# Forward attention of a gated recurrence sent through DRAM and added to the backward one, so that one product with the values serves both directions

## The chip, the core and the metric

The kernel runs on one core of a Trainium2 chip. The engines are named as in the profile: PE (TensorE, matrix products), PEld (its weight loads), DVE (VectorE), ACT (ScalarE), POOL (GpSimd) and SP (SyncE, which here issues nearly all DMA transfers). The metric is the device time of one execution in microseconds (us); lower is better.

## What is computed

One layer of a block with two recurrent branches over 2048 latent tokens and 256 context tokens, model width 1024. The change lies in the second branch (HGRN2, branch B), which has 4 heads of width 128 and runs over the sequence in both directions; the outputs of the two directions are added:

```python
def step(S, inp):                       # one chunk of one direction
    qg_c, attn_c, v_c, kd_c, gl_c = inp
    o_c = einsum('bhcd,bhdv->bhcv', qg_c, S) + einsum('bhcs,bhsv->bhcv', attn_c, v_c)
    S = S * gl_c[..., :, None] + einsum('bhcd,bhcv->bhdv', kd_c, v_c)
    return S, o_c
...
for d in range(2):                      # forward, then backward
    o_c, o_l = prefix_scan(gla_chunk_scan, ctx_args, lat_args, s0_b, reverse=(d == 1))
    ob_lat_cm = ob_lat_cm + o_l
```

Within a chunk the output is a part from the state S that came in, and a part `attn . v` from the chunk's own tokens. `attn` is lower triangular in the forward direction and upper triangular in the backward one; v is the same in both. So attn_forward . v + attn_backward . v = (attn_forward + attn_backward) . v.

## The kernel before

The program has these stages in order of time: the modulated input (0 to 170 us of the span), the projections with convolution of branch A (to about 500 us), the whole of branch B (about 500 to 1046 us), the preparation of branch A's chunks (to about 1450 us), branch A's recurrence (to about 1700 us), and the output with its projections and normalisation (to the end). Gate projections, which depend on nothing in the recurrences, are spread among the last three. All projections are products of 128 x 512 tiles in float32r, each done as three products of high and low halves (lines L216 to L218, tile `ps`).

Branch B is the function `scan_group(h, d, g, ps, S)`, called per head h (4), direction d (0 forward, 1 backward) and group g of 512 tokens: four latent groups and one context group of 256 tokens (g = 4), which comes first in both directions and has no output. The chunk is 128 tokens, so a latent group has k_ = 4 of them, index i. One latent group does, in short: gates on ACT and DVE (tiles `s`, `sn`, `X`; the running sum is L546, with the mask `m32` as one operand), scaled queries and keys `ag`, `bg`, `a64`, `b64`, `b32` (L601 and L619 on DVE, L604, L620, L621 on POOL), the transposed keys `pk` and `kd`, the state updates' products `pS` (L614), the chunk's attention in 32 x 32 and 32 x 64 pieces into the PSUM tile `pat` (L625, L627), and then

- L647, DVE: the allowed triangle of `pat` is copied into `atB[d]`, an SBUF tile per direction whose other triangle is zero;
- L655, PE: `pw` = queries times state S (queries `ag` forward, `bg` backward);
- L656, PE: `pw` += `atB[d]` times v, four products of 128 x 128 in float32;
- L661, DVE: the next state, in a ring of four tiles of tag "S";
- forward: ACT copies `pw` to `o` (L664), and SP stores it to the DRAM tensor `oP` (L665); backward: SP loads `oP` into `o` (L650), DVE adds `pw` (L667), and SP stores the sum (L668).

A group's values v are loaded from DRAM into the single tile `v` (L588), the queries into the single tile `q` (L591). Between groups, `head_units` (values and queries of the next head) and `gate_units` are called as filling; their projections are what PE does while a group's chain runs on the other engines.

The order of the instructions on each engine isn't the order of the code: a scheduler (`schedule_with_timeline_sim=True`) simulates the program while it is built and lays down each engine's list. Each engine then executes its list strictly in order, and so does SP with its DMA issues: an instruction that waits holds up all that stand behind it on its engine. Tiles come from pools; a tile that is used again waits for the last reader of its earlier use.

Of the kernel before, what the change touches and what calls it, by code (L numbers as in the profile page):

```python
# [8 lines left out]
F32 = mybir.dt.float32  # L9
F32R = mybir.dt.float32r  # L10
U8 = mybir.dt.uint8
AF = mybir.ActivationFunctionType
ALU = mybir.AluOpType
# [3 lines left out]
P = 128  # L17
# [7 lines left out]
H = 4  # L25
# [3 lines left out]
NG = SEQ // GT  # L29
# [10 lines left out]
def block_kernel(ctx, tc, x, c, ctx_in, c_ctx, w_mod, b_mod, w_in, conv_w, a_log, dt_bias,  # L40
                 lb_param, a_norm_g, b_norm_g, w_a_out, w_b_out, w_out, ln_g, ln_b, out, dbg=None):
    nc = tc.nc
    sy, te, ve, ac, po = nc.sync, nc.tensor, nc.vector, nc.scalar, nc.gpsimd
# [43 lines left out]
    dr = ctx.enter_context(tc.tile_pool(name="dr", reuse_waits="tile", bufs=1, space=DRAM))  # L87
# [62 lines left out]
    qB = dr.tile([H, NG, P, GT], F32, name="qB")  # L150
    vB = dr.tile([H, NG + 1, P, 4, P], F32, name="vB")
    oP = dr.tile([H, NG, P, 4, P], F32, name="oP")
    oBD = dr.tile([SEQ // P, P, H, P], F32, name="oBD")
    gateD = dr.tile([1, D], F32, name="gateD")
    gT = dr.tile([24, P, SEQ], F32, name="gT")
# [55 lines left out]
    def proj(w, gi, pool=None, tag="pj"):  # L211
        wh, wl = w
        n = GT if gi < NG else CTX
        ps = (pool or pj[0]).tile([P, n], F32, tag=tag, name="ps")
        for k in range(KB):
            te.matmul(out=ps, lhsT=wh[:, k, :], rhs=uhi[gi][:, k, :], start=(k == 0), stop=False)  # L216
            te.matmul(out=ps, lhsT=wh[:, k, :], rhs=ulo[gi][:, k, :], start=False, stop=False)  # L217
            te.matmul(out=ps, lhsT=wl[:, k, :], rhs=uhi[gi][:, k, :], start=False, stop=(k == KB - 1))  # L218
        return ps
# [15 lines left out]
    with tc.tile_pool(name="w0", reuse_waits="tile", bufs=1, side="right") as w0, \  # L235
# [85 lines left out]
        for k in range(KB):  # L321
            if k in (0, 2):
                w_part(w0_, gcol[0], 2 * k)
            for j in range(2):
# [4 lines left out]
                for i in range(2):  # L329
                    te.matmul(out=pm[2 * j + i], lhsT=sc[:, k, :], rhs=wm[:, i * 512:i * 512 + 512],  # L330
                              start=(k == 0), stop=(k == KB - 1))
# [176 lines left out]

    with tc.tile_pool(name="rb", reuse_waits="tile", bufs=1, side="right") as rb, \
            tc.tile_pool(name="pb", reuse_waits="tile", bufs=1, space=PSUM) as pb:  # L510
        m32 = rb.tile([P, 256], F32, name="m32")
        po.memset(m32, 1.0)
        po.memset(m32.rearrange("p (b t) -> p b t", t=32)[:, :, 0:1], 0.0)
        mk = [rb.tile([P, P], U8, name=f"mk{d}") for d in range(2)]
        atB = [rb.tile([P, 4, P], F32, name=f"atB{d}") for d in range(2)]
# [6 lines left out]
        def bl(a):  # L522
            return slice(32 * a, 32 * a + 32)

        def b4(t):
            return t.rearrange("p c (b t) -> p c b t", t=32)

        def scan_group(h, d, g, ps, S):
# [25 lines left out]
            else:  # L554
                ve.tensor_tensor(out=X3[:, :, 1:32], in0=s3[:, :, 0:31],
                                 in1=s3[:, :, 15:16].to_broadcast([P, nb, 31]), op=ALU.subtract)
# [30 lines left out]
            v = rb.tile([P, 4, P], F32, tag="v", name="v")  # L587
# [7 lines left out]
            def fb(f, m):  # L595
                return f.unsqueeze(3).to_broadcast([P, k_, m, 32])
# [18 lines left out]
            if lat:  # L615
                a64 = rb.tile([P, 4, 64], F32, tag="a64", name="a64")
                b64 = rb.tile([P, 4, 64], F32, tag="b64", name="b64")
                b32 = rb.tile([P, 4, 64], F32, tag="b32", name="b32")
                ve.tensor_tensor(out=b4(a64), in0=b4(a)[:, :, 2:4], in1=fb(f2, 2), op=ALU.mult)  # L619
                po.tensor_tensor(out=b4(b64), in0=b4(b)[:, :, 0:2], in1=fb(f3, 2), op=ALU.mult)  # L620
                po.tensor_tensor(out=b4(b32), in0=b4(b)[:, :, 0:4:2], in1=fb(f4, 2), op=ALU.mult)  # L621

                def mm(i, am, bm, asl, bsl):
                    if d == 0:
                        te.matmul(out=pat[bsl, i, asl], lhsT=bm, rhs=am, start=True, stop=True)  # L625
                    else:
                        te.matmul(out=pat[asl, i, bsl], lhsT=am, rhs=bm, start=True, stop=True)  # L627


                def across32(i, k):  # L630
                    mm(i, a[:, i, bl(2 * k + 1)], b32[:, i, bl(k)], bl(2 * k + 1), bl(2 * k))

                def across64(i, k):
                    if d == 0:
                        mm(i, a64[:, i, :], b64[:, i, bl(k)], slice(64, 128), bl(k))
                    else:
                        mm(i, a64[:, i, bl(k)], b64[:, i, :], bl(2 + k), slice(0, 64))

                for i in range(4):
                    for k in range(4):  # L640
                        mm(i, a[:, i, bl(k)], b[:, i, bl(k)], bl(k), bl(k))
                for i in range(4):
                    across32(i, d)
                    across32(i, 1 - d)
                    across64(i, d)
                    across64(i, 1 - d)
                ve.copy_predicated(out=atB[d], mask=mk[d].unsqueeze(1).to_broadcast([P, 4, P]), data=pat)  # L647
                o = rb.tile([P, 4, P], F32, tag="o", name="o")
                if d == 1:
                    sy.dma_start(out=o, in_=oP[h, g])  # L650
                pw = pb.tile([P, 4, P], F32, tag="o", name="pw")
                qg = ag if d == 0 else bg
            for i in (range(k_) if d == 0 else range(k_ - 1, -1, -1)):
                if lat:
                    te.matmul(out=pw[:, i, :], lhsT=qg[:, i, :], rhs=S, start=True, stop=False)  # L655
                    te.matmul(out=pw[:, i, :], lhsT=atB[d][:, i, :], rhs=v[:, i, :], start=False, stop=True)  # L656
                S2 = rb.tile([P, P], F32, tag="S", name="S2", bufs=4)
                if S is None:
                    ve.tensor_copy(out=S2, in_=pS[:, i, :])
                else:  # L660
                    ve.scalar_tensor_tensor(out=S2, in0=S, scalar=fz[:, i, 14:15], in1=pS[:, i, :], op0=ALU.mult, op1=ALU.add)  # L661
                S = S2
            if lat and d == 0:
# [43 lines left out]
        for h in range(H):  # L707
            fill = head_units(h + 1) if h + 1 < H else gate_units(NEARLY + GA)
            for d in range(2):
                w = load_w((C_FF, C_FB)[d] + h * P)  # L710
                S = None
                for j, g in enumerate(((4, 0, 1, 2, 3), (4, 3, 2, 1, 0))[d]):
                    S = scan_group(h, d, g, proj(w, g), S)
                    for _ in range(FBI[d][j] if h + 1 < H else FB[j] * d):
                        next(fill, None)
            for _ in fill:
                pass
# [18 lines left out]
    with tc.tile_pool(name="rc", reuse_waits="tile", bufs=2, side="right") as rc, \  # L736
# [8 lines left out]
        for d in range(2):  # L745
            po.tensor_copy(out=after[d].rearrange("p (h t) -> p h t", h=H),
                           in_=(m_lt, m_gt)[d].bitcast(F32).unsqueeze(1).to_broadcast([P, H, P]))
# [192 lines left out]
    if True:  # L940
# [9 lines left out]
        def stepA(d, ch, lat, second, last):  # L950
# [14 lines left out]
            def mm4(lhs, rhs):  # L965
                cnt[0] += 1
                two = cnt[1] >= SW and cnt[0] % 3
                ps = (pd2 if two else pd).tile([P, H, P], F32, tag="A", name="psA")
                for h in range(H):
                    te.matmul(out=ps[:, h, :], lhsT=lhs[:, h, :], rhs=rhs[:, h, :], start=True, stop=True)  # L970
                return ps

            def tok_scale(tag, ps, sc_):
                t = rd.tile([P, H, P], F32, tag=tag, name=tag)
                for h in range(H):
                    ac.activation(out=t[:, h, :], in_=ps[:, h, :], func=AF.Copy, scale=sc_[:, d, ch, h:h + 1])
                return t
# [7 lines left out]
            if not last:  # L985
                pS = mm4(kn, tok_scale("vx", pv, nbze))
                S2 = rd.tile([P, H, P], F32, tag=f"S{d}", name="S2")
                for h in range(H):
                    ve.scalar_tensor_tensor(out=S2[:, h, :], in0=S[:, h, :], scalar=gl[:, d, ch, h:h + 1], in1=pS[:, h, :],  # L989
                                            op0=ALU.mult, op1=ALU.add)  # L990
                SA[d] = S2
            if lat:
# [242 lines left out]
```

## Time and profile before

| what | us |
|---|---|
| median of 3 runs | 2251.22 (2248.89 to 2253.9) |
| the profiled execution | 2248.18 |
| its span, first to last instruction | 2246.4 |
| PE busy in it | 2134.7 (95%) |
| DVE, ACT, POOL busy | 1395.4 (62%), 927.1 (41%), 655.3 (29%) |
| DMA engines, hardware queue | 48.0% of 16 engines' span |

The profile is one execution. "Busy" is the time in which an engine has an instruction of the program in execution. Records of matrix products overlap one another (each is in flight for longer than the distance to the next one), so the distance between two starts is what one costs PE; a product in float32 shows as two records. Names stand as out<-in without buffer numbers. The lines of the profile are shown in the prediction, at the place where each is used.

### The profile page before, as it was taken

The numbers are of one execution on the slowest core, as the hardware profiler recorded it, in microseconds if no ns is written. First come the engines' busy times: TensorE is split into PE (matmuls) and PEld (weight loads), VectorE is DVE, ScalarE is ACT, GpSimd is POOL, SyncE is SP. The second block draws the span as 40 slices with busy tenths as digits, with TensorE's granted clock in tenths as the row PEclk, the third lists the DMA queues.
The fourth block names the chain that finished last, engine by engine and source line by source line (L and its number), as shares of the span: only waits on it lengthen the run. The fifth ranks groups of instructions, "written<-read, shape, count | busy, mean of one in ns | idle before, by whom it ended". The sixth has DMA issues, their size and how long they took to land. (4 is left out here: it accounts for less than half of the span.)

```text
span 2246.4 us, 40304 instructions
## 1 busy us (share of the span) xinstructions
PE 2134.7 (95%) x15184; PEld 1786.2 (80%) x15184; DVE 1395.4 (62%) x3225; ACT 927.1 (41%) x2334; POOL 655.3 (29%) x656
## 2 busy tenths in 40 slices
PE   8999999999999999999998898999989888999998
PEld 3778888888888888888777677788778877888887
DVE  5836666627776777784698887733332338666664
ACT  4623222224443443443455554344444445444441
POOL 3413343312221222223333332211133224423331
PEclk9999999999999999999999999999999999999999
DMA  8312222322322323225778887777878864444432
GB/s 338 109 39 71 68 73 69 92 71 69 97 83 76 106 69 97 83 86 160 237 221 234 246 242 203 241 208 223 236 260 288 267 210 154 141 137 127 140 95 80
DMA packets 303670, 339.77 MB, mean 151 GB/s; under 512 B 78124, under 2 KB 217650, under 8 KB 303476
## 3 DMA queue, kind: packets, MB, share of 16 engines
q1 hardware_dynamic: 301459, 329.87, 48.0%
q0 software_dynamic: 2016, 7.34, 0.9%
q8 instruction: 119, 1.95, 0.4%
q14 instruction: 76, 0.61, 0.1%
HBM read 226.27 MB, written 110.87 MB: 150 GB/s over the span
## 5 line engine op out<-in xcount | busy, mean ns | idle before, releaser
L216 PE MATMUL ps<-uhi,wh 128*128 128x512 f32 (+1 forms) x1824 | 708.4, 388 | 4.2 <-DVE uhi L305 2.0
L217 PE MATMUL ps<-ulo,wh 128*128 128x512 f32 (+1 forms) x1824 | 708.0, 388 | 2.9 <-DVE ulo L310 1.7
L218 PE MATMUL ps<-uhi,wl 128*128 128x512 f32 (+1 forms) x1824 | 707.3, 388 | 0.7 <-POOL wl L203 0.7
L216 PEld LDWEIGHTS ps<-uhi,wh 128*128 128x128 f32 x1824 | 346.3, 190 | 68.5 <-DVE uhi L305 3.0
L217 PEld LDWEIGHTS ps<-ulo,wh 128*128 128x128 f32 x1824 | 346.1, 190 | 66.2 <-DVE ulo L310 2.5
L218 PEld LDWEIGHTS ps<-uhi,wl 128*128 128x128 f32 x1824 | 346.2, 190 | 63.3 <-POOL wl L203 1.1
L203 POOL TENSOR_TENSOR wl<-ws,wh 128x512 fp32r<-128x512 f32 x144 | 192.8, 1339 | 590.5 <-ACT wh L202 575.1
L202 ACT CAST wh<-ws 128x512 fp32r<-128x512 f32 x144 | 89.3, 620 | 292.8 <-DMA ws<-in_w_in_dram 214.3
L418 DVE SCALAR_TENSOR_TENSOR acc<-raw,cols,acc 128x512 f32<-128x512 f32 x192 | 153.9, 854 | 0.9
L1134 PE MATMUL py<-yh,wab 128*128 128x256 f32 x512 | 145.0, 284 | 7.5 <-DVE mg L1137 6.0
L1135 PE MATMUL py<-yl,wab 128*128 128x256 f32 x512 | 144.4, 282 | 1.4 <-POOL yl L1117 1.4
L1136 PE MATMUL py<-yh,wab 128*128 128x256 f32 x512 | 143.7, 281 | 0.0
L604 POOL TENSOR_TENSOR bg<-s,fz 128x512 f32<-128x512 f32 (+1 forms) x36 | 37.5, 1041 | 260.9 <-ACT X L584 106.7
L1153 PE MATMUL pso<-uhi,mh 128*128 128x512 f32 x256 | 102.9, 403 | 8.0 <-ACT mh L1139 4.1
L1134 PEld LDWEIGHTS py<-yh,wab 128*128 128x128 f32 x512 | 96.8, 190 | 10.0 <-DVE mg L1137 7.4
L1155 PE MATMUL pso<-uhi,ml 128*128 128x512 f32 x256 | 101.8, 398 | 0.6 <-DVE ml L1140 0.6
L1154 PE MATMUL pso<-ulo,mh 128*128 128x512 f32 x256 | 101.4, 397 | 0.0
L1135 PEld LDWEIGHTS py<-yl,wab 128*128 128x128 f32 x512 | 97.0, 189 | 2.3 <-POOL yl L1117 1.8
L1136 PEld LDWEIGHTS py<-yh,wab 128*128 128x128 f32 x512 | 97.5, 190 | 0.1
L989 DVE SCALAR_TENSOR_TENSOR S<-S,gl,psA 128x128 f32<-128x128 f32 x136 | 38.2, 341 | 87.0 <-PE psA L970 87.0
L1117 POOL TENSOR_TENSOR yl<-gt,yh 128x512 fp32r<-128x512 f32 x32 | 44.9, 1405 | 147.4 <-ACT yh L1116 147.4
L1127 ACT ACTIVATE mg<-mg 128x512 f32<-128x512 f32 x64 | 40.4, 632 | 112.2 <-DMA mg<-gT 106.5
(373 smaller groups left out, 3963.1 us busy)
## 6 DMA issues: line engine op xcount, KB each, us to landing
ws<-in_w_in_dram SPq DMA_DIRECT2D x144, 256.0 KB, 3.0
gT<-gt SPq DMA_DIRECT2D x96, 256.0 KB, 4.4
kv<-knvD SPq DMA_DIRECT2D x36, 512.0 KB, 5.9
kq<-qkvD SPq DMA_DIRECT2D x32, 512.0 KB, 5.5
an<-atN SPq DMA_DIRECT2D x32, 512.0 KB, 6.2
mg<-gT SPq DMA_DIRECT2D x64, 256.0 KB, 3.4
qkvD<-acc SPq DMA_DIRECT2D x48, 256.0 KB, 2.3
l<-qkvD SPq DMA_DIRECT2D x16, 768.0 KB, 6.1
```

The lines of the kernel that those rows point to most:

```text
L202: ac.copy(out=wh[:, j:j + 4, :], in_=ws)
L203: po.tensor_tensor(out=wl[:, j:j + 4, :], in0=ws, in1=wh[:, j:j + 4, :].bitcast(F32), op=ALU.subtract)
L216: te.matmul(out=ps, lhsT=wh[:, k, :], rhs=uhi[gi][:, k, :], start=(k == 0), stop=False)
L217: te.matmul(out=ps, lhsT=wh[:, k, :], rhs=ulo[gi][:, k, :], start=False, stop=False)
L218: te.matmul(out=ps, lhsT=wl[:, k, :], rhs=uhi[gi][:, k, :], start=False, stop=(k == KB - 1))
L418: ve.scalar_tensor_tensor(out=a_, in0=raw[:, o + k:o + k + n], scalar=wk, in1=a_, op0=ALU.mult, op1=ALU.add)
L1134: te.matmul(out=py[:, i, :], lhsT=wh[:, k, ms_], rhs=yh[i][:, k, :], start=(k == 0), stop=False)
L1135: te.matmul(out=py[:, i, :], lhsT=wh[:, k, ms_], rhs=yl[i][:, k, :], start=False, stop=False)
L1136: te.matmul(out=py[:, i, :], lhsT=wl[:, k, ms_], rhs=yh[i][:, k, :], start=False, stop=(k == H - 1))
L1153: te.matmul(out=ps, lhsT=mh[:, k, ts_], rhs=wout[0][k][:, ns], start=(k == 0), stop=False)
L1154: te.matmul(out=ps, lhsT=mh[:, k, ts_], rhs=wout[1][k][:, ns], start=False, stop=False)
L1155: te.matmul(out=ps, lhsT=ml[:, k, ts_], rhs=wout[0][k][:, ns], start=False, stop=(k == KB - 1))
```

## The change

In the forward direction the product `atB[0]` . v is left out: `pw` holds the state's part alone. Instead SP stores `atB[0]` to a new DRAM tensor `atF` (256 KB for each of 16 head and group pairs). In the backward direction SP loads it into a new tile `at`, POOL adds `atB[1]` to it in place, and PE multiplies the sum with v. To make room for `at`, the mask `m32` becomes uint8 and the ring of states has three tiles in place of four.

```diff
+    atF = dr.tile([H, NG, P, 4, P], F32, name="atF")
...
-        m32 = rb.tile([P, 256], F32, name="m32")
+        m32 = rb.tile([P, 256], U8, name="m32")
...
                 ve.copy_predicated(out=atB[d], mask=mk[d].unsqueeze(1).to_broadcast([P, 4, P]), data=pat)
+
+                if d == 0:
+                    sy.dma_start(out=atF[h, g], in_=atB[0])
+                else:
+                    at = rb.tile([P, 4, P], F32, tag="at", name="at")
+                    sy.dma_start(out=at, in_=atF[h, g])
+                    po.tensor_tensor(out=at, in0=at, in1=atB[1], op=ALU.add)
                 o = rb.tile([P, 4, P], F32, tag="o", name="o")
...
             for i in (range(k_) if d == 0 else range(k_ - 1, -1, -1)):
                 if lat:
-                    te.matmul(out=pw[:, i, :], lhsT=qg[:, i, :], rhs=S, start=True, stop=False)
-                    te.matmul(out=pw[:, i, :], lhsT=atB[d][:, i, :], rhs=v[:, i, :], start=False, stop=True)
-                S2 = rb.tile([P, P], F32, tag="S", name="S2", bufs=4)
+                    te.matmul(out=pw[:, i, :], lhsT=qg[:, i, :], rhs=S, start=True, stop=d == 0)
+                    if d == 1:
+                        te.matmul(out=pw[:, i, :], lhsT=at[:, i, :], rhs=v[:, i, :], start=False, stop=True)
+                S2 = rb.tile([P, P], F32, tag="S", name="S2", bufs=3)
```

The new lines make all later line numbers larger: up to L645 by one, then more. The product with v is L665 in the changed kernel (L656 before), the product with the state L663 (L655), the state update L670 (L661), the addition on POOL L655, the store and the load of `atF` L651 and L654.

The scheduler lays the lists down anew. Only the stage of branch B and the stages of branch A's preparation and the first half of its recurrence come out in another order; what is ahead of branch B, and the rest of the recurrence and the output, stand as before. Three places are shown.

PE, a forward group of the first head, around the products with the state. `ps` is projection work of another unit, `S2` the states. Before:

```order
L218 MATMUL ps_4414<-uhi3_634,wl_3892 128x512
L655 MATMUL pw_4084<-S2_4087,ag_4028 128x128
L656 MATMUL pw_4084<-v_4023,atB0_3558 128x128
L655 MATMUL pw_4084<-S2_4091,ag_4028 128x128
L656 MATMUL pw_4084<-v_4023,atB0_3558 128x128
L655 MATMUL pw_4084<-S2_4095,ag_4028 128x128
L656 MATMUL pw_4084<-v_4023,atB0_3558 128x128
L625 MATMUL pat_3560<-X_4130,s_4128 32x32
L609 MATMUL pk_4166<-ident_60,bg_4164 128x128 x4
```

PE at the same place, now:

```order
L218 MATMUL ps_4406<-ulo3_636,wh_3892 128x512
L663 MATMUL pw_4086<-S2_4088,ag_4029 128x128
L219 MATMUL ps_4406<-uhi3_635,wl_3893 128x512
L217 MATMUL ps_4406<-uhi3_635,wh_3892 128x512
L663 MATMUL pw_4086<-S2_4091,ag_4029 128x128
L626 MATMUL pat_3561<-X_4128,s_4126 32x32
L663 MATMUL pw_4086<-S2_4094,ag_4029 128x128
L626 MATMUL pat_3561<-X_4128,s_4126 32x32 x2
L610 MATMUL pk_4164<-ident_60,bg_4162 128x128 x4
```

The products with v are gone from between the products with the states, and pieces of projection and attention stand there in their place.

POOL, the second and third backward group of the first head. `wl` is the low half of projection weights, which needs ACT's high half and that in turn a weight load; `b64`, `b32` and `bg` are scaled operands of the group. Before:

```order
L604 TENSOR_TENSOR bg_4930<-s_4893,fz_4896 128x512
L620 TENSOR_TENSOR b64_4945<-s_4893,fz_4896 128x256
L621 TENSOR_TENSOR b32_4946<-s_4893,fz_4896 128x256
L203 TENSOR_TENSOR wl_5176<-ws_5181,wh_5175 128x512
L604 TENSOR_TENSOR bg_5101<-s_5064,fz_5067 128x512
L620 TENSOR_TENSOR b64_5116<-s_5064,fz_5067 128x256
L621 TENSOR_TENSOR b32_5117<-s_5064,fz_5067 128x256
```

POOL at the same place, now:

```order
L655 TENSOR_TENSOR at_4975<-at_4975,atB1_3560 128x512
L204 TENSOR_TENSOR wl_5455<-ws_5456,wh_5454 128x512
L605 TENSOR_TENSOR bg_5096<-s_5059,fz_5062 128x512
L621 TENSOR_TENSOR b64_5111<-s_5059,fz_5062 128x256
L622 TENSOR_TENSOR b32_5112<-s_5059,fz_5062 128x256
L204 TENSOR_TENSOR wl_5455<-ws_5460,wh_5454 128x512
L655 TENSOR_TENSOR at_5149<-at_5149,atB1_3560 128x512
```

The addition of the second group follows straight on that group's operands; that of the third stands behind a `wl`. Of the 16 additions 5 stand straight behind a `wl`.

DVE, the end of a backward group of the second head, with its four state updates. Before:

```order
L661 SCALAR_TENSOR_TENSOR S2_6379<-S2_6222,fz_6287,pS_6330 128x128
L661 SCALAR_TENSOR_TENSOR S2_6383<-S2_6379,fz_6287,pS_6330 128x128
L661 SCALAR_TENSOR_TENSOR S2_6387<-S2_6383,fz_6287,pS_6330 128x128
L661 SCALAR_TENSOR_TENSOR S2_6391<-S2_6387,fz_6287,pS_6330 128x128
L562 MEMSET fz_6629 128x4
L546 SCALAR_TENSOR_TENSOR s_6455<-m32_3553,s_6455 128x256 x2
```

The end of that list now, from the next group's last preparing step on (the first three updates stand 15 to 18 rows ahead of it):

```order
L584 TENSOR_TENSOR X_6449<-X_6449,sn_6448 128x512
L594 TENSOR_TENSOR s_6447<-q_6479,s_6447 128x512
L670 SCALAR_TENSOR_TENSOR S2_6383<-S2_6379,fz_6276,pS_6319 128x128
L676 TENSOR_TENSOR o_6366<-o_6366,pw_6368 128x512
L602 TENSOR_TENSOR ag_6482<-X_6449,fz_6450 128x512
```

The fourth update has moved behind nearly all of the next group's gate work: with three tiles its tile is free only after PE's second product with a state of that group.

## The prediction

> **What bounds the kernel now.** I began with the busy time by stage, since the change lies in one of them. In a row of this view stand the stretch in us, its length, then for each engine its busy time and, in brackets, its instructions; at the end TensorE's granted clock, the DMA engines' busy share and GB/s. The first row is branch B, the second branch A's preparation, the third the recurrence.
>
> ```profile
> 514.00:1046.00 532.00, 526.84 (x4714) 446.17 (x4713) 381.51 (x1039) 217.60 (x396) 131.47 (x136) 1.00 0.30 89
> 1046.00:1450.00 404.00, 365.23 (x2686) 298.27 (x2685) 316.31 (x842) 198.94 (x659) 124.76 (x148) 0.96 0.78 232
> 1450.00:1700.00 250.00, 233.02 (x2251) 197.56 (x2249) 85.41 (x263) 110.26 (x350) 53.32 (x70) 0.97 0.77 235
> ```
>
> In branch B PE is without work for 5 us of 532, at the full clock. DVE is busy for 72% of it, POOL for 25%, the DMA engines for 30%. So a product that PE is spared there should be time gained, as long as PE goes on finding work. Busy records of PE overlap, though, so I looked next at what a product costs from start to start, in the timeline (start, duration, line):
>
> ```profile
> 521.39 0.40 PE L217 MATMUL ps<-ulo,wh 128*128 128x512 f32 x1
> 521.63 0.38 PE L656 MATMUL pw<-v,atB 128*128 128x128 f32 x2
> 521.77 0.48 PE L218 MATMUL ps<-uhi,wl 128*128 128x512 f32 x1
> 522.08 0.40 PE L216 MATMUL ps<-uhi,wh 128*128 128x512 f32 x1
> 522.32 0.40 PE L217 MATMUL ps<-ulo,wh 128*128 128x512 f32 x1
> ...
> 523.47 0.38 PE L655 MATMUL pw<-S,ag 128*128 128x128 f32 x2
> 523.69 0.39 PE L656 MATMUL pw<-v,atB 128*128 128x128 f32 x2
> 523.92 0.39 PE L655 MATMUL pw<-S,ag 128*128 128x128 f32 x2
> 524.14 0.39 PE L656 MATMUL pw<-v,atB 128*128 128x128 f32 x2
> ```
>
> In a row of float32 products each starts 0.22 to 0.23 us after the one before. Between projections it costs the same: from 521.39 to 522.08 are 0.69 us, of which two projection products at 0.23 are 0.46, which leaves 0.23 for the one of L656. PE is issuing without a gap, and this is the price.
>
> Then the stage by halves of a head, forward (first and third row and so on) and backward in turn, in stretches of 70 us:
>
> ```profile
> 500.00:570.00 70.00, 70.00 (x623) 60.04 (x622) 51.26 (x160) 31.65 (x59) 13.18 (x15) 1.00 0.24 73
> 570.00:640.00 70.00, 70.00 (x611) 59.29 (x610) 50.62 (x121) 27.65 (x49) 19.51 (x18) 1.00 0.36 104
> 640.00:710.00 70.00, 68.85 (x615) 58.61 (x615) 49.31 (x152) 31.26 (x58) 13.70 (x15) 1.00 0.22 69
> 710.00:780.00 70.00, 70.00 (x611) 59.27 (x610) 49.07 (x114) 27.69 (x50) 19.50 (x18) 1.00 0.34 100
> 780.00:850.00 70.00, 68.18 (x607) 58.14 (x606) 50.34 (x150) 30.20 (x57) 13.65 (x15) 0.98 0.24 73
> 850.00:920.00 70.00, 70.00 (x611) 59.28 (x610) 50.37 (x126) 28.48 (x51) 19.51 (x18) 1.00 0.34 99
> 920.00:990.00 70.00, 67.81 (x649) 56.30 (x648) 59.29 (x170) 32.16 (x60) 16.39 (x18) 1.00 0.24 72
> ```
>
> All that PE misses, it misses in the forward stretches, 1.15, 1.82 and 2.19 us of the third, fifth and seventh row. That is where the products go away. The backward stretches are full, and there the new addition comes in. Last, who waits for whom in the stage (total us, times, longest):
>
> ```profile
> PE pw L655 <- DVE S L661: 2.7, 3, 1.3
> PEld pw L655 <- DVE S L661: 2.5, 2, 1.4
> POOL wl L203 <- ACT wh L202: 119.0, 22, 12.4
> DVE S L661 <- PE pS L614: 11.7, 15, 2.6
> ```
>
> PE's waits on the states come to 5.2 us, nearly all that it waits for; POOL stands for long before a `wl`.
>
> **The change part by part.** *Forward products left out.* 4 heads x 4 groups x 4 chunks are 64 products, half of those in this row (two records each):
>
> ```profile
> L656 PE MATMUL pw<-v,atB 128*128 128x128 f32 x256 | 49.5, 275 | 0.0
> ```
>
> 64 x 0.223 us = 14.3 us less of PE's time. The mean of 275 ns in the row is flight time, which overlaps; it isn't the price. The page "Perfetto Trace Analysis" of the Trainium skill, section "Identifying the Most-Contended Engine", would have PE judged by its weight loads' busy share and not by the products': here 446.17 of 532 us, 84%, so by this rule PE had room and sparing it would bring less. The timeline disagrees: a 512-wide product takes 0.23 us and its load 0.19, so loads can't fill such a stretch while the products do:
>
> ```profile
> L216 PEld LDWEIGHTS ps<-uhi,wh 128*128 128x128 f32 x1824 | 346.3, 190 | 68.5 <-DVE uhi L305 3.0
> ```
>
> *The store and load of `atF`, the addition, `v`.* The nearest rows:
>
> ```profile
> L997 POOL TENSOR_TENSOR o<-o,part 128x512 f32<-128x512 f32 x16 | 20.4, 1276 | 53.3 <-ACT o L976 22.3 <-DMA part<-oAD 12.7 <-DVE r L982 4.7
> L647 DVE COPY_PREDICATED atB<-mk,pat x32: 718/735/747, 518.0 to 1026.9; 128x512 f32<-128x512 uint8 x32
> v<-vB SPq DMA_DIRECT2D x32, 256.0 KB, 2.7
> oP<-o SPq DMA_DIRECT2D x16, 256.0 KB, 3.2
> L650 SPq DMA_DIRECT2D o<-oP x16: 319/320/332, 564.1 to 1030.0; - x16
> ```
>
> L997 is the same operation, in place, on the same shape: 1.28 us. Sixteen are 20.4 us on POOL, in backward stretches where POOL is busy 19.5 of 70. What they stand before is PE's first product with v. In the new order some 17 projection products, four transposes and four products for the state lie between the group's last piece of attention and it: 17 x 0.23 + 8 x 0.2 = 5.5 us. The chain takes 0.74 (L647) + 1.28, with a few tenths for semaphores 2.4 us. Cover is left, 3 us: 0. Without cover it would be 16 x 2.4 = 38 us at most, 0 at least. The load waits, like that of `v` ahead of it on SP, for the last product of the group before; 0.64 us of two issues and 2.7 to land are 3.4 us, and PE comes back to that place after about 12 us: 0. The store makes the next group's L647 wait until it has landed, 0.32 + 3.2 us of a group period of over 10: 0. SP issues 32 transfers more, 32 x 0.32 = 10 us in 532, and 8.4 MB more move at 30% DMA load: 0. The first backward group reads what the last forward one wrote; the context group lies between: 0.
>
> POOL's additions can also stretch DVE. Of these two products, each with two operands in SBUF, the second is always the same, while the first, which runs beside POOL's scaling, goes up to 1.58 us (its minimum is the half size):
>
> ```profile
> L601 DVE TENSOR_TENSOR ag<-X,fz x36: 425/831/1581, 512.5 to 1020.0; 128x512 f32<-128x512 f32 x32, 128x256 f32<-128x256 f32 x4
> L593 DVE TENSOR_TENSOR X<-q,X x16: 676/684/695, 510.3 to 961.1; 128x512 f32<-128x512 f32 x16
> ```
>
> 16 additions x (1.58 - 0.68) = 14 us of DVE at most, 3.6 us in each backward stretch, where DVE has 20 us to spare: 0 on the path. The page "SBUF — State Buffer", section "Who interferes with whom", says that such a DVE instruction and a GpSimd one that reads SBUF lock each other out for a whole instruction; the trace agrees, 1.58 against 0.68 us.
>
> *The mask as uint8.* L546 with a float32 mask, and the scan of branch A, which has a uint8 operand and twice the length:
>
> ```profile
> L546 DVE TENSOR_TENSOR_SCAN s<-m,s x72: 658/682/950, 500.0 to 1013.3; 128x256 f32<-128x256 f32 x72
> L797 DVE TENSOR_TENSOR_SCAN dec<-gb,after x36: 1198/1225/1868, 1048.3 to 1365.6; 128x512 f32<-128x512 f32 x36
> ```
>
> 1225 ns for twice 682 less one fixed part: no dearer. 0, bounds 0 to 72 x 0.05 = 4 us of DVE.
>
> *Three states in place of four.* The fourth update of a group must wait for PE's second product with a state, and stands later on DVE; PE's first product of the next group waits for it. Backward some 7 us of other PE work lie between, forward only the attention pieces and four transposes, about 2 us, for one update of 0.34 us and what DVE has in hand. Lower bound 0, upper bound that the present 5.2 us of waits double, +5.2. I take +2.6: the forward cover is thin and DVE's work in a stretch stays while PE's shrinks by 3.6 us.
>
> *Order in the preparation and recurrence.* PE does the same work there, in another order, and waits 38.8 us of 404, in waits such as these:
>
> ```profile
> PE pkk L805 <- ACT kv L769: 9.6, 8, 1.8
> PE pk L766 <- DMA l<-qkvD: 5.1, 4, 1.6
> ```
>
> That is some 40 waits of 1 us. If each falls anew the sum moves by about the root of 40, 6 us, either way. I take 0, bounds -6 and +6.
>
> *Sum.* -14.3 + 0 + 2.6 + 0 = -11.7 us. The profiled execution took 2248.18 us (span 2246.4 and 1.8 around it), 3.0 less than the median of the runs, so it goes to 2236.5 and the median to 2239.5.
>
> **The rivals.** *A, the spared time becomes waiting.* In the forward stretches the chain over DVE and ACT is close behind: PE already misses 1 to 2 us in three of four there, and the seventh row has DVE busy for 59 of 70. If the chain sets the pace of a forward half, PE's 14.3 us are idle in place of busy: 0 to -4, time about 2249. For it: all waits lie there. Against: DVE has 19 to 21 us to spare in the other rows, and filling work exists. The rule on weight loads above would lead here as well.
>
> *B, the addition is late (slower).* POOL's list puts 5 of 16 additions straight behind a `wl`, and such an instruction has waited up to 12.4 us, 5.4 in the mean, with all behind it. If those five came late by 5.4 us more than the 3 us of cover, and all others by 1, then 27 + 11 - 14.3 = +24 us, 2275. It decides from 0.9 us of wait a backward group (14.3 / 16). For it: the long row. Against: most of those waits are POOL with nothing else to do, and the `wl` ahead of an addition is the second half of a load, whose weights tile is free already.
>
> *C, the new order behind branch B.* It costs 12 us or more in the two later stages, twice what I allow: 2251 or above; or it brings as much, 2227 or less. The trace of before can't say.
>
> **How the numbers follow.** The forecast, -5 to -19 us, has 0.62. A has 0.14 (within 0.2%, 4.5 us, which is about what a measurement of this kernel can tell from no change, as its three runs lie within 5.0 us). B 0.07. C with a cost 0.09, of which 0.04 still comes out slower and 0.05 the same; C with a gain 0.08. So faster 0.62 + 0.08 + 0.01 of the edges = 0.71, same 0.14 + 0.05 - 0.01 = 0.18, slower 0.07 + 0.04 = 0.11. The range: 2227 is 2251.2 - 14.3 - 6 and a run's spread of 4; 2253 takes in A and the mild side of C, and leaves out B. The likeliest case alone: 2232 to 2246.
>
> **What would show it.** Right: branch B's stage some 10 to 14 us shorter, PE's products of L665 half as many as L656's, PE still without work for under 2% of the stage; POOL's additions at 1.28 us with no PE wait on them; the stretch behind branch B as long as now within 6 us. Wrong: PE waiting on `S` of L670 or on ACT's and DVE's gate steps for over 8 us (A), PE waiting on `at` (B), or the preparation longer by more than was gained (C).

## The result, and the profile after

| what | us |
|---|---|
| changed kernel, median of 6 runs | 2232.98 (2229.54 to 2237.38) |
| kernel before beside it, median of 6 runs | 2250.05 (2245.27 to 2253.9) |
| ratio after / before | 0.9932 [0.9916, 0.9948] |
| profiled executions, before and after | 2248.18 and 2233.26 (spans 2246.4 and 2231.6) |

The change makes the kernel 15.3 us faster (11.7 to 18.9 by the interval; the two medians lie 17.1 us apart, within it); forecast were 11.7. The sum came out near. Two of its terms did not, and they partly cancel, which is luck.

The busy time by stage, in the same columns as in the prediction, cut at the same events in both kernels: branch B from its first attention piece to its last `pw`, then the middle (branch A's preparation and the start of its recurrence, up to its last product of `lvt`), the rest of the recurrence, and the output. Before:

```profile
514.50:1039.40 524.90, 519.74 (x4680) 440.31 (x4680) 380.17 (x1036) 216.40 (x393) 125.89 (x127) 1.00 0.30 88
1039.40:1637.30 597.90, 551.29 (x4630) 453.50 (x4628) 384.55 (x1051) 284.50 (x930) 163.01 (x208) 0.97 0.77 228
1637.30:1812.00 174.70, 156.79 (x1016) 141.50 (x1013) 54.14 (x164) 75.38 (x245) 54.33 (x43) 0.96 0.81 267
1812.00:2246.40 434.40, 405.45 (x2530) 358.93 (x2529) 274.08 (x452) 175.07 (x476) 142.47 (x97) 0.99 0.42 134
```

and after:

```profile
515.50:1028.70 513.20, 503.22 (x4533) 424.23 (x4533) 389.86 (x1036) 215.16 (x393) 152.46 (x148) 0.99 0.34 106
1028.70:1626.70 598.00, 549.59 (x4648) 452.49 (x4648) 384.85 (x1051) 283.77 (x930) 162.76 (x204) 0.98 0.76 229
1626.70:1797.90 171.20, 153.77 (x1016) 139.29 (x1013) 54.47 (x165) 75.04 (x245) 54.34 (x43) 0.98 0.83 271
1797.90:2231.60 433.70, 406.90 (x2530) 360.52 (x2529) 274.36 (x452) 175.59 (x476) 143.44 (x97) 0.98 0.42 134
```

Branch B is 11.7 us shorter, just the forecast, what comes behind it 4.1 us shorter, what is ahead 1.0 longer. But the stage doesn't hold the same work: some projections have moved behind it. The same stretches for the first of the three projection lines alone (L216 before, L217 after) show how many:

```profile
514.50:1039.40 524.90, 209.03 (x547) 102.92 (x546) 1.00 0.30 88
```

```profile
515.50:1028.70 513.20, 207.38 (x541) 102.13 (x540) 0.99 0.34 106
```

Six or seven fewer of that line, so about 20 fewer of the three lines, at the 0.23 us from start to start that the prediction read: 4.6 us. At equal work branch B gained 11.7 - 4.6 = 7.1 us, about half of what the spared products are worth, and the middle gained 4.5.

What took the other half? PE is busy for 503.22 of 513.20 us, so it is without work for 10.0 us against 5.2 before, and the granted clock is 0.99 against 1.00. PE's waits on others, after (total us, times, longest; a wait shows only where a releaser is seen):

```profile
PE pat L626 <- POOL b L622: 1.9, 3, 0.8
PE pw L663 <- DVE S L670: 1.7, 2, 1.0
PE pk L610 <- POOL bg L605: 1.7, 3, 1.0
PE pS L615 <- DMA v<-vB: 1.6, 1, 1.6
```

and before:

```profile
PE pw L655 <- DVE S L661: 2.7, 3, 1.3
PE pk L609 <- POOL bg L604: 0.9, 1, 0.9
PE pat L625 <- ACT s L577: 0.9, 1, 0.9
```

The wait on the states went down, with three tiles. What came are waits on POOL's operands, 3.6 us against 0.9, and, in rows not shown, 3.7 us on DVE's `ag` and on the load of `v`, against 0.6. And the clock drops near some of the pauses. PE at the start of the second head, after, in slices of 5 us (length, busy, granted clock, DMA share, GB/s):

```profile
645.00:650.00 5.00, 5.00 (x29) 1.00 0.01 3
650.00:655.00 5.00, 2.87 (x47) 0.88 0.34 107
655.00:660.00 5.00, 5.00 (x47) 0.50 0.01 4
660.00:665.00 5.00, 5.00 (x25) 0.94 0.45 157
```

PE misses 2.1 us, and in this slice and the next two it gets less than its clock: 0.12 + 0.50 + 0.06 of 5 us, 3.4 us more. So the clock that is lost around a pause can be more than the pause itself. The page "TensorE: Matmul & The Clock Gate" of the Trainium skill, section "Part 1: The HAM clock gate", tells of a clock halved after an idle window of some 3.4 us, until a busy one of that length; the row with 0.50 agrees with the half, and 3.4 x 0.5 = 1.7 us, by that page an estimate, is the loss of a single drop here (0.66 in a slice of 5 us). Here drops stand behind pauses of about 2 us, shorter than such a window (2.1 us here, 1.8 in the last section).

### The profile page after: what moved, and what is told of

Read it like the earlier page. It is cut to its first block, busy times and chain, and to the rows that moved or that the text cites. A ratio compares the mean times of both kernels' runs of the same rounds, so it can differ in the third digit from the quotient of the medians.

```text
span 2231.6 us, 40198 instructions
## 1 busy us (share of the span) xinstructions
PE 2114.9 (95%) x15056; PEld 1767.6 (79%) x15056; DVE 1404.9 (63%) x3225; ACT 925.3 (41%) x2334; POOL 688.2 (31%) x672
## 5 line engine op out<-in xcount | busy, mean ns | idle before, releaser
L217 PE MATMUL ps<-uhi,wh 128*128 128x512 f32 (+1 forms) x1824 | 708.2, 388 | 2.9 <-DVE uhi L306 2.6
L217 PEld LDWEIGHTS ps<-uhi,wh 128*128 128x128 f32 x1824 | 345.7, 190 | 66.4 <-DVE uhi L306 3.9
L204 POOL TENSOR_TENSOR wl<-ws,wh 128x512 fp32r<-128x512 f32 x144 | 200.2, 1391 | 551.7 <-ACT wh L203 494.4
## 6 DMA issues: line engine op xcount, KB each, us to landing
kv<-knvD SPq DMA_DIRECT2D x36, 512.0 KB, 5.1
kq<-qkvD SPq DMA_DIRECT2D x32, 512.0 KB, 6.0
an<-atN SPq DMA_DIRECT2D x32, 512.0 KB, 6.2
```

The lines of the kernel that those rows point to most:

```text
L204: po.tensor_tensor(out=wl[:, j:j + 4, :], in0=ws, in1=wh[:, j:j + 4, :].bitcast(F32), op=ALU.subtract)
```

## The experiments

All ratios are to the kernel before, run on the same chip, with 95% intervals. Two sizes are read from each profile's branch B besides its length, summed over slices of 5 us: PE without work, and clock loss, each slice's length times one less the granted clock. The table of all kernels stands behind the last group.

### Parts of the change alone

**Ring and mask alone.**

```diff
-        m32 = rb.tile([P, 256], F32, name="m32")
+        m32 = rb.tile([P, 256], U8, name="m32")
...
-                S2 = rb.tile([P, P], F32, tag="S", name="S2", bufs=4)
+                S2 = rb.tile([P, P], F32, tag="S", name="S2", bufs=3)
```

> The kernel before with only the two space-saving edits: the mask m32 as uint8 and the ring of states of three tiles. Theory 1 (the gain is PE time of the 64 products left out, the rest of the change is hidden): no work is spared, so 0 to +5 us against the kernel before, branch B's stage 525 to 530 us from the first attention product to the last product of pw (525 before). Rival (part of the gain comes from the shorter ring or the new order that it brings): -3 us or more.

Measured: 1.0021 [1.0008, 1.0033], 4.7 us slower.

**The change with four states.** The changed kernel, with the ring as before; `stack2` is laid into the tile `sqt` for the room.

```diff
-    stack2 = cp.tile([32, 16], F32, name="stack2")
+    sqt = cp.tile([P, SEQ // P, H], F32, name="sqt")
+    stack2 = sqt[0:32].rearrange("p g h -> p (g h)")[:, 0:16]
...
-    sqt = cp.tile([P, SEQ // P, H], F32, name="sqt")
...
-                S2 = rb.tile([P, P], F32, tag="S", name="S2", bufs=3)
+                S2 = rb.tile([P, P], F32, tag="S", name="S2", bufs=4)
```

> The changed kernel with the ring of states back at four tiles (the small constant stack2 is laid into the later tile sqt to make room). Theory 1: DVE's wait for PE at the state update (8.3 us in the changed kernel) goes, PE's own waits on the states stay near 3 us, the time is that of the changed kernel within 4 us, so -12 to -19 us against the kernel before. Rival (the shorter ring costs PE as priced, 2.6 us or more): 3 to 5 us faster than the changed kernel, -18 to -22.

Measured: 0.9992 [0.9979, 1.0005], no gain that is clear of noise. Both ranges missed.

**Only the spared products.** The kernel before, without the forward products.

```diff
-                    te.matmul(out=pw[:, i, :], lhsT=qg[:, i, :], rhs=S, start=True, stop=False)
-                    te.matmul(out=pw[:, i, :], lhsT=atB[d][:, i, :], rhs=v[:, i, :], start=False, stop=True)
+                    te.matmul(out=pw[:, i, :], lhsT=qg[:, i, :], rhs=S, start=True, stop=d == 0)
+                    if d == 1:
+                        te.matmul(out=pw[:, i, :], lhsT=atB[d][:, i, :], rhs=v[:, i, :], start=False, stop=True)
```

> The kernel before with the 64 forward products with v left out and nothing put in their place: no store, no load, no addition, ring of four, float32 mask. It leaves the forward direction's attention part out of the result. Theory 1: this is the bare saving, 14.3 us less in branch B's stage (511 us against 525), -12 to -19 us in all, the same as the changed kernel within 4 us. Rival A (the spared time becomes waiting): -4 us or less. Rival B (the way over DRAM and POOL costs the changed kernel time): 5 us or more faster than the changed kernel, -20 or beyond.

Measured: 0.9945 [0.9925, 0.9965], 12.4 us faster.

**Only the costs.** The changed kernel, with the forward products kept.

```diff
-                    te.matmul(out=pw[:, i, :], lhsT=qg[:, i, :], rhs=S, start=True, stop=d == 0)
-                    if d == 1:
-                        te.matmul(out=pw[:, i, :], lhsT=at[:, i, :], rhs=v[:, i, :], start=False, stop=True)
+                    te.matmul(out=pw[:, i, :], lhsT=qg[:, i, :], rhs=S, start=True, stop=False)
+                    te.matmul(out=pw[:, i, :], lhsT=(at if d else atB[0])[:, i, :], rhs=v[:, i, :], start=False, stop=True)
```

> The changed kernel with the forward products kept: store, load, addition, short ring and uint8 mask are there, the 64 products too, so the forward attention part is counted twice in the result. Theory 1: all that the change adds is hidden, 0 to +4 us against the kernel before, branch B's stage 525 to 529 us. Rival B: +8 us or more, with PE waiting on at.

Measured: 1.0001 [0.9986, 1.0015].

These don't add up: the costs alone cost nothing, ring and mask alone cost 4.7 us, and with four states the gain is gone. The stages tell why. Branch B and the middle, ring and mask alone, then the change with four states:

```profile
514.60:1041.60 527.00, 521.44 (x4691) 442.27 (x4691) 382.56 (x1037) 216.59 (x395) 127.07 (x128) 1.00 0.29 88
1041.60:1647.00 605.40, 553.43 (x4636) 456.31 (x4634) 389.96 (x1054) 283.99 (x932) 161.40 (x207) 0.96 0.74 226
```

```profile
514.90:1037.20 522.30, 514.03 (x4574) 432.07 (x4573) 388.48 (x1037) 216.31 (x396) 149.78 (x144) 0.99 0.34 105
1037.20:1639.70 602.50, 548.95 (x4607) 451.35 (x4607) 382.91 (x1051) 281.37 (x928) 162.78 (x207) 0.97 0.75 226
```

Set to the projections that the kernel before has in branch B, ring and mask alone leave branch B as it was (524.7 us) and lengthen the middle by 9.8. The change with four states shortens branch B by 7.7, about as the changed kernel does (7.1), and loses 9.7 in the middle. There both kernels do the same work as before in another order. Only the spared products (branch B -16.7, middle +1.3) and only the costs (+2.5 and +5.3) go the same way. So, by one profiled execution of each, the middle moves the time by as much as the change itself, and the changed kernel drew a good order (-4.5). The change's own worth can't be had this way.

### With the order behind branch B held

A barrier of all engines at the end of branch B, in every kernel of this group, keeps the scheduler from mixing the stages. Behind it PE's list is the same row for row in all of them, and branch B holds the same projections. The ratios are still to the kernel before, without a barrier.

```diff
     uC.close()
+    tc.strict_bb_all_engine_barrier()
```

**Before, the change, the change with four states, and only the spared products, each with the barrier.**

> The kernel before with a barrier of all engines between branch B and branch A's preparation. Behind it the scheduler's order no longer depends on what stands in branch B: TensorE's list behind the barrier is the same, row for row, in this kernel and the three that follow, so that their differences are branch B's own. The barrier itself may cost 0 to +15 us against the kernel before; no theory differs here.

> The changed kernel with the same barrier. Theory 1 (the spared products shorten branch B, and the order behind it added or took some us by chance): 8 to 14 us less than the fenced kernel before. Theory 2 (branch B gains little, and the gain of the changed kernel is mostly the order that the scheduler found behind it): 0 to 5 us less.

> The changed kernel with the ring of states of four and the same barrier. Without the barrier this ring took away the whole gain, and the profile puts that behind branch B (543 to 555 us from the last product of pw to the last of lvt at equal projections against the changed kernel's). Theory 1: with the order behind held, it is equal to the fenced changed kernel within 3 us. Rival (the ring of four does harm in branch B itself): 8 us or more slower than the fenced changed kernel.

> The kernel before without the forward products with v, nothing in their place (the forward attention part is missing from the result), with the same barrier. Theory 1 (64 products at 0.223 us, all of it gained): 14 to 17 us less than the fenced kernel before; what the fenced changed kernel falls short of it is the price of store, load, addition and short ring, priced at 2.6 us in the prediction. Rival A (part of the spared time turns into waits): 8 us or less.

Measured, in this order: 1.0101 [1.0083, 1.0119], 1.0068 [1.0056, 1.0080], 1.0101 [1.0082, 1.0120], 1.0049 [1.0030, 1.0068]. Branch B in the four:

```profile
516.90:1035.70 518.80, 510.26 (x4635) 432.17 (x4635) 378.69 (x1036) 214.06 (x389) 120.49 (x123) 1.00 0.27 86
```

```profile
516.20:1027.70 511.50, 501.36 (x4509) 422.87 (x4507) 384.26 (x1036) 213.75 (x389) 144.28 (x139) 0.99 0.32 103
```

```profile
514.00:1030.60 516.60, 500.33 (x4507) 420.90 (x4507) 386.60 (x1036) 212.56 (x389) 143.64 (x139) 0.99 0.32 102
```

```profile
515.00:1018.90 503.90, 496.80 (x4508) 418.29 (x4507) 380.99 (x1036) 213.49 (x389) 121.11 (x123) 1.00 0.28 88
```

The spared products alone give 14.9 us of branch B (11.7 +- 5.9 in the times). The whole change gives 7.3 (7.4 +- 4.9 in the times), as it does without a barrier; that is between the ranges of both theories. So store, load and addition, which were priced at nothing, with ring and mask take back about 7 by the profiles; between the times of these two kernels the difference is 4.3 +- 5.0 us, not clear of nothing. With four states it isn't equal within 3 us, as was expected, but 5.1 longer in branch B: the ring of three isn't what costs. PE's waits in the change with the barrier:

```profile
PE pw L665 <- POOL at L655: 2.4, 2, 1.9
PE pk L610 <- POOL bg L605: 2.0, 4, 1.0
PE pw L663 <- DVE S L670: 1.7, 2, 1.0
PE pat L626 <- POOL b L622: 1.6, 2, 0.8
```

6.0 us of these are on POOL, where the additions themselves wait for 47.8 us, with all that stands behind them:

```profile
POOL at L655 <- DVE atB L648: 17.7, 5, 5.0
POOL at L655 <- PE pt L688: 15.8, 4, 4.0
POOL at L655 <- DMA at<-atF: 14.3, 4, 4.1
```

That gave the theory for the last group: the cost is the addition's place on POOL, in order with `b`, `bg` and `wl`, and not the load, the product or the ring. Its rival was that PE waits for `at` itself.

**The addition on DVE.** With the barrier, and without:

```diff
-                    po.tensor_tensor(out=at, in0=at, in1=atB[1], op=ALU.add)
+                    ve.tensor_tensor(out=at, in0=at, in1=atB[1], op=ALU.add)
```

> The changed kernel with the addition of at on DVE, right behind the copy of the attention, and the barrier behind branch B. Theory 1 (the price in branch B, 7.5 us between the fenced changed kernel and the fenced kernel without the products, is POOL: its list stands before the additions, and PE waits 6 us on POOL's at, bg and b): those waits of PE fall to 2 to 3 us, branch B's stage from 511.4 to 505 to 508 us. Theory 2 (the price is the shorter ring and DVE): 11 us more on DVE make it 511 us or longer.

> The changed kernel with the addition on DVE, without the barrier: whether it beats the changed kernel. Theory 1 gives branch B 3 to 6 us less than the changed kernel at equal projections; the order behind branch B is drawn anew, worth -4 to +10 us in the kernels so far, so -8 to -22 us against the kernel before, or nothing if the order falls badly.

**Spared products with a ring of three and the mask**, without store, load and addition: the kernel before with the barrier, only the products spared as above, and

```diff
-        m32 = rb.tile([P, 256], F32, name="m32")
+        m32 = rb.tile([P, 256], U8, name="m32")
...
-                S2 = rb.tile([P, P], F32, tag="S", name="S2", bufs=4)
+                S2 = rb.tile([P, P], F32, tag="S", name="S2", bufs=3)
```

> The kernel before without the forward products, with the ring of three and the uint8 mask, and the barrier; no store, load or addition, so the forward attention part is missing from the result. Theory 1: the ring costs next to nothing, branch B's stage 503 to 506 us (503.9 with the ring of four and float32 mask). Theory 2: 509 to 512 us, as in the fenced changed kernel.

**The sum made and not read.** The change with the barrier, where PE multiplies `atB[1]` and not `at`:

```diff
-                        te.matmul(out=pw[:, i, :], lhsT=at[:, i, :], rhs=v[:, i, :], start=False, stop=True)
+                        te.matmul(out=pw[:, i, :], lhsT=atB[1][:, i, :], rhs=v[:, i, :], start=False, stop=True)
```

> The fenced changed kernel with store, load and addition, but PE multiplies atB[1] and not at with v, so that PE doesn't wait for the addition; the forward attention part is missing from the result. Theory 1: the additions still stand in POOL's list and hold up what is behind, so branch B's stage is 507 to 511 us, with PE waits on bg and b of 3 us or more. Rival (only PE's own wait for at costs): 504 to 506 us.

Measured: addition on DVE with the barrier 1.0041 [1.0024, 1.0058], without it 0.9927 [0.9909, 0.9945]; ring and mask with the spared products 1.0031 [1.0018, 1.0043]; sum not read 1.0061 [1.0043, 1.0080]. Branch B of the three with the barrier, addition on DVE, no addition, sum not read:

```profile
515.20:1021.10 505.90, 498.95 (x4508) 420.75 (x4507) 388.27 (x1052) 214.48 (x389) 119.63 (x123) 0.99 0.33 105
```

```profile
516.70:1016.60 499.90, 495.54 (x4507) 418.50 (x4507) 381.04 (x1036) 214.47 (x389) 122.40 (x123) 1.00 0.29 89
```

```profile
515.10:1019.20 504.10, 496.05 (x4507) 418.60 (x4507) 388.90 (x1036) 213.35 (x389) 144.38 (x139) 1.00 0.33 105
```

On DVE the addition gives back 5.6 us of branch B (6.1 +- 4.7 in the times). Without store, load and addition the rest of the change is 11.6 us shorter than with them (8.3 +- 3.9 in the times), and shorter than the 503 to 506 us that were expected. So between half and three quarters of the price hangs on the addition's being on POOL, 5.6 of 11.6 or of the 7.6 us that the change lies above only the spared products. Store, load and an addition on DVE still cost 6.0 us of branch B (2.2 +- 4.7 in the times). The kernel that makes the sum and doesn't read it fell in the rival's range by its branch B (504.1, 7.4 below the change), but by the times it is no more than 1.6 +- 5.0 us faster. The table shows the reason for the difference: 5.5 of those 7.4 us are clock loss in the one profiled execution. So whether PE's wait on `at` has a share of its own isn't settled. Without a barrier the version on DVE can't be told from the changed kernel (0.9927 against 0.9932, the intervals overlap); no version was shown to beat it.

### All kernels, branch B

"Equal" is the length set to the projections of the kernel before, at 0.23 us each (behind a barrier they are equal anyway); the last column is that length less PE without work and clock loss.

| kernel | branch B | equal | PE without work | clock loss | remainder |
|---|---|---|---|---|---|
| before | 524.9 | 524.9 | 5.2 | 1.7 | 518.0 |
| ring and mask alone | 527.0 | 524.7 | 5.5 | 1.7 | 517.5 |
| only the costs (addition on POOL) | 532.5 | 527.4 | 8.7 | 0.0 | 518.7 |
| only the spared products | 513.3 | 508.2 | 3.1 | 0.0 | 505.2 |
| changed kernel (POOL) | 513.2 | 517.8 | 10.0 | 3.4 | 504.4 |
| change, four states (POOL) | 522.3 | 517.2 | 8.2 | 3.4 | 505.6 |
| change, addition on DVE | 512.0 | 512.2 | 6.0 | 1.7 | 504.5 |
| barrier: before | 518.8 | | 8.5 | 1.4 | 508.9 |
| barrier: only the spared products | 503.9 | | 7.1 | 1.7 | 495.1 |
| barrier: spared products, ring, mask | 499.9 | | 4.4 | 1.7 | 493.8 |
| barrier: change (POOL) | 511.5 | | 10.1 | 7.2 | 494.2 |
| barrier: change, four states (POOL) | 516.6 | | 16.3 | 5.2 | 495.1 |
| barrier: sum not read (POOL) | 504.1 | | 8.1 | 1.7 | 494.3 |
| barrier: addition on DVE | 505.9 | | 6.9 | 4.5 | 494.5 |

The remainder knows only two values in each group, with the 64 products and without: 518.07 and 504.93 in the mean without a barrier, 508.9 and 494.5 with it. That is 13.1 and 14.4 us, the spared products and nothing else. All the rest of the differences is PE without work and the clock that drops around it. Without an addition PE misses 5.6 us in the mean of six kernels (3.1 to 8.5), with it on POOL 10.2 (8.1 to 16.3), with it on DVE 6.0 and 6.9. The clock loss goes from 1.4 to 3.5 in the mean with the addition on POOL, very unevenly: each is one execution. Together about 6.7 us stand against the addition on POOL, with a wide spread: with the barrier the three kernels that have it there are 0.2, 7.6 and 12.7 us longer than only the spared products. With it on DVE the clock loss is 1.7 and 4.5 us, so it is the time without work, and not the clock, that tells DVE from POOL.

## Why the prediction was right, and where it wasn't

*Forward products, -14.3.* Right in kind and size: 13.1 and 14.4 us by the remainder, 0.20 to 0.23 us a product. PE busy falls by 13.5 us from the kernel before to the one with only the products spared, both with the barrier (510.26 and 496.80). The rule of the Trainium skill's page "Perfetto Trace Analysis", section "Identifying the Most-Contended Engine", by which PE had room, is not borne out: loads filled 440.31 of 524.90 us of branch B before, and the products' price still came out whole.

*Store, load, addition, 0.* This term failed; it stands at about +6.7 us, and its sizes were not the reason. The addition in the changed kernel, its load's issue and its load's landing:

```profile
L655 POOL TENSOR_TENSOR at<-at,atB x16: 1271/1384/1731, 576.7 to 1021.3; 128x512 f32<-128x512 f32 x16
L654 SPq DMA_DIRECT2D at<-atF x16: 319/424/497, 557.0 to 1017.3; - x16
DMA to landing us min/median/max: 2.9/3.8/4.3
```

1.38 us for the 1.28 of the nearest row, 3.8 for 2.7. And the cover held nearly everywhere: in the changed kernel no wait of PE on `at` shows, with the barrier 2.4 us of two. The step that failed is "cover is left, 3 us: 0". It counted only the product behind the addition, and not what else stands behind it in POOL's list.

```profile
L655 POOL TENSOR_TENSOR at<-at,atB 128x512 f32<-128x512 f32 x16 | 22.3, 1393 | 54.9 <-PE pt L688 15.7 <-DVE atB L648 13.5 <-DMA at<-atF 8.2
```

55 us of POOL's idle time lie just ahead of the 16 additions, but most of it holds nothing up. Behind twelve additions POOL is idle again, for 0.5 to 6.9 us, until the next instruction's own operands come; behind a thirteenth the next one was ready only as the addition ended. The other three are the last additions of the first three heads, at 627, 768 and 904 us. A `wl` starts as each of them ends, 1.0, 1.2 and 1.1 us after its own last wait, by the semaphores in the trace. This is the first (start, duration, engine, line; in brackets the idle time before it and what ended that):

```profile
626.48 0.62 ACT L203 CAST wh<-ws 128x512 fp32r<-128x512 f32 x1 [0.39 <-PE ps L218]
627.36 1.27 POOL L655 TENSOR_TENSOR at<-at,atB 128x512 f32<-128x512 f32 x1 [4.08 <-DVE atB L648]
628.59 1.47 POOL L204 TENSOR_TENSOR wl<-ws,wh 128x512 fp32r<-128x512 f32 x1
633.62 0.62 ACT L203 CAST wh<-ws 128x512 fp32r<-128x512 f32 x1 [2.65 <-DMA ws<-in_w_in_dram]
634.14 0.38 ACT L539 ACTIVATE s<-ps 128x256 f32<-128x256 f32 x1
651.54 1.05 POOL L605 TENSOR_TENSOR bg<-s,fz 128x512 f32<-128x512 f32 x1 [8.92 <-ACT fz L574]
```

The weights come through the single tile `ws`, whose last reader is `wl`. So the next load waits for the held `wl`, ACT waits 2.65 us for that load, and the gates of the next head (`s`, later `fz`) stand behind it on ACT. POOL then waits for ACT, and PE for POOL's `bg`: the pause at 650 us stands at the end of this chain. The same rows stand ahead of the pauses near 791 and 930 us. With only the products spared, and no barrier, the same `s` starts at 630.6 us and PE has no such pause; so the hold of 1.0 us is part of what makes it late, not all.

It fits with where PE's time is missed. Cut at the last `pw` of each direction, 7.5 of the changed kernel's 10.0 us lie in forward stretches, which have no addition. In the mean PE misses 3.9 us there in the kernels without an addition and 7.4 with it on POOL (4.0 and 4.6 with it on DVE); in the backward stretches it is 1.7 and 2.8 (2.0 and 2.4). That the held `wl` is the whole price isn't shown. With the barrier and the addition on DVE no `wl` is held at 627 us, and PE still misses 1.4 us near 650, against 1.7 with it on POOL. Every kernel also gets its own lists, so the move to DVE changes more than the addition's place. Rival B had part of it: it named POOL's list and `wl`, but had the addition wait behind a `wl`, where the trace has a `wl` waiting behind the addition.

*Ring of three, +2.6, and mask, 0.* Not seen as a cost in branch B. The upper bound was read too high: its 5.2 us add the waits of PE (2.7) and of its weight loads (2.5) on the states, which are for the most part the same ones. PE without work goes from 5.2 to 5.5, 8.2 to 10.0, 7.1 to 4.4 and 16.3 to 10.1 us from four states to three. PE's waits on `S` are 1.7 us after and 2.7 before. The scan with a uint8 mask takes 722 ns where it took 689:

```profile
L547 DVE TENSOR_TENSOR_SCAN s<-m,s 128x256 f32<-128x256 uint8 x72 | 49.6, 722 | 27.6 <-ACT s L545 27.3
```

72 x 33 ns are 2.4 us of DVE, within the bounds given.

*Order in the preparation and recurrence, 0 +- 6.* The middle differs by -4.5 to +9.8 us at equal work over the six kernels without a barrier, so the bounds were too narrow. In the changed kernel the middle gave -4.5 us, the rest of the recurrence -3.5 and the output -0.7. Summed over slices of 5 us, PE without work behind branch B is 93.5 us before and 92.6 after, but the clock loss is 32.7 and 24.4: 8 us more of granted clock. (The PEclk of the stage rows shows it roughly: 0.97, 0.96, 0.99 before, 0.98, 0.98, 0.98 after.) The last two stages have the same order in both kernels, so what they differ by is one execution against another, or what came before. The times say the same: -15.3 in all, of which branch B's -7.1 leave some -8.

*The sum.* -14.3 + 6.7 in place of -14.3 + 2.6 for branch B, that is -7.6 against -7.1 measured, and about -8 behind it in place of 0. The forecast of -11.7 lay between what the change itself is worth and what this build of it measured; its range held both. That it came within 4 us is luck: a cost that was put at nothing and a gain behind branch B that was put at nothing came out at nearly the same size. Of the signs named, L665 has half the records (128 for 256), PE is without work for 1.9% of the stage, just under the 2% named, and the gain of branch B is 10 to 14 us only as long as the moved projections are counted.

*Rival A* didn't come about: with only the products spared PE misses less than before (3.1 for 5.2 us; with the barrier 7.1 for 8.5). *Rival C* did in part, on the side of a gain.

## What to carry to other kernels

On a full in-order engine an instruction spared is worth its distance from start to start, and this held to a tenth over fourteen kernels once waits and clock were taken off. An instruction added to a half-idle engine isn't priced by its duration and its own reader alone: look in that engine's list for what stands right behind it and is ready, as the `wl` here, and for who waits on that. Here the addition cost less on DVE, right behind the copy that it waits for. Where a scheduler lays all later work anew, hold that order in both kernels (a barrier at the stage's end) before a part of the change is priced; here the middle alone differed by -5 to +10 us at equal work, as much as the change is worth.

## What the runs showed that had not been expected

A pause of PE of about two microseconds can be followed by a loss of clock of the same size, and needn't be. With the same barrier the kernel before missed 2.7 us at one place and kept its clock:

```profile
795.00:800.00 5.00, 2.33 (x44) 1.00 0.33 108
800.00:805.00 5.00, 5.00 (x57) 1.00 0.04 5
```

while without it a pause of 1.8 us at the same place was followed by 0.66:

```profile
790.00:795.00 5.00, 3.18 (x40) 1.00 0.27 96
795.00:800.00 5.00, 5.00 (x64) 0.66 0.04 12
```

What decides it isn't shown here. From branch B to the end the clock loss is 34.4 us before and 27.8 after, so at a few drops of 1.7 us more or less two executions differ by as much as the parts of this change.
